# Sums for the second feed-forward layer made and stored in the first, and the embedding's projection moved to the head of the first layer

## The chip, the cores and the metric

The kernel runs on one core of one Trainium2 chip. The metric is the device time of one execution in microseconds (us), as the median of several runs. A profile of one execution gives the instructions of each engine: TensorE (PE: matmuls, PEld: weight loads), VectorE (DVE), ScalarE (ACT), GpSimd (POOL) and SyncE (SP, which here issues every transfer between HBM and SBUF).

## What is computed

An encoder layer over two sequences of 1024 tokens with 1024 features, in float32. Cut to the part that the change touches (attention and the state-space mixer come before it):

```python
h = h + mix @ w_out                                   # "out" product
f = rms_norm(h, g_mlp)
h = h + jnp.square(jax.nn.relu(f @ w_mlp1)) @ w_mlp2  # layer 1 (1024 -> 4096), layer 2 (4096 -> 1024)
e = rms_norm(h, g_ple)
h = h + jax.nn.sigmoid(e @ w_ple_gate) * (p_i @ w_ple_proj)   # gate, and the embedding's projection
return rms_norm(h, g_final)
```

## The kernel before

The two sequences go through three phases. The first two (in-projection, state-space mixer, attention, and a gated unit) take the first 938 us and are not touched. The third, class `PhaseC`, is run once for each sequence, s = 0 and then s = 1, in this order: out product, layer 1, layer 2, gate with the embedding's projection, last norm and output.

**Matmuls in three parts.** Each float32 operand is split into a high and a low part, `hi` by a cast on ACT (L1228), `lo = x - hi` on DVE or POOL (L1229), and a product is made of three matmuls, hi·hi, hi·lo and lo·hi (L461, L462, L463). `split` writes to small buffers of the pool `ops`, three for each of four names, so splits run at most three steps ahead of the matmuls.

**Strassen's products.** Layer 1 goes through eight chunks (`layer1`, ch = 0 to 7) of 512 of the 4096 hidden features. A chunk is seven products of 24 matmuls instead of eight, by the scheme of Strassen and Winograd. The right sides are the normalised activations: half 0 of the tokens directly, and the sums `T` of both halves, which `Sums` makes as the norm of half 1, `norm(h, gb, o, 1)`, comes through transposes on PE (n_ps, L561). In chunk 0 this norm is emitted behind the chunk's first two products (matmuls mz<-act), which need half 0 alone. Each output z (128x1024) is an add on DVE (L1341), a relu (L1346) and a square (L1347) on ACT and a store of 512 KB.

Layer 2 (`strassen`) takes the chunks in pairs (0,1), (2,3), (4,5): a pair is seven products of 48 matmuls; chunk 6 alone is seven of 24, and chunk 7 is plain, 192 matmuls, with the norm for the gate behind it. For a pair, four blocks of hidden values (left, `hid`, 1 MB each) and four of weights (right, `wr`) are loaded; the left sides' four sums are made on DVE and the right sides' four on POOL (L1264), each in two instructions of 128x1024 elements, in place, between the products. DVE also splits the left sides and adds the finished products into h and u2 (L1386, L1395); POOL also splits the right sides.

**The embedding's projection** (pj): p is transposed and split while chunk 7 of layer 2 runs; its 96 matmuls, for each sequence, stand between those of the gate, six for each bank of 128x512. The gate's sigmoid is multiplied by the bank of pj in PSUM (L1537) and added to h (L1538).

**Order.** A scheduler puts each engine's instructions into one order at build time, and each engine then goes through its own in that order. All transfers are issued by SP in one order over eight completion semaphores. `K(R[i], ...)` is one of 16 named places of 8 KB per partition, each with a single tenant at a time; the pool `t2` has two buffers, `up` two, `raw` three, `wp` four, and PSUM's eight banks are split into pm1 (three) and pm2 (five).

Of the kernel before, what the change touches and what calls it, by code (L numbers as in the profile page):

```python
# [16 lines left out]
P = 128  # L17
# [958 lines left out]
class Glu:  # L976


    def __init__(self, nc, tc, ctx, io, ident, ones, scr, B, cols):
        self.nc, self.io, self.ident, self.ones, self.scr, self.B = nc, io, ident, ones, scr, B  # L980

        def pool(name, bufs, **k):
            return ctx.enter_context(tc.tile_pool(name=name, bufs=bufs, reuse_waits="tile", side="right", **k))
        self.one = pool("G1", 1)
        self.two = pool("G2", 2)
        self.cols = cols
        self.w = self.one.tile([P, 4, 512], F32, name="wglu")
        nc.sync.dma_start(out=self.w, in_=io["w_glu"].rearrange("(k p) c -> p k c", p=P))
        self.gt, self.halves = {}, 0
        B.tasks += [self.gelu(), self.unit(0)]  # L990

    def gelu(self):
# [4 lines left out]
        for s in range(2):  # L997
            self.gt[s] = []
            for f in range(4):
                yt = self.two.tile([P, 8, NCK], F32, tag="yt", name="yt")  # L1000
                with B.tc.high_priority(offset=FIRST_AHEAD if s == 0 and f < 2 else 0):
                    nc.sync.dma_start(out=yt, in_=scr["y"][8 * f:8 * f + 8, :, :, s].rearrange("g h t c -> (g h) t c"))
# [177 lines left out]
class PhaseC:  # L1180
# [72 lines left out]
    def strassen(self, A, s1, B, t2, read):  # L1253

        v, g = self.nc.vector, self.nc.gpsimd
        odd = [False]  # L1260

        def op(e, out, x, y, how=ALU.subtract):
            for k in range(0, out.shape[1], 2):
                e.tensor_tensor(*(z[:, k:k + 2] for z in (out, x, y)), op=how)  # L1264

        def product(i, a, b):
            read(i, self.product([a], [b], odd[0]))
            odd[0] = not odd[0]
        product(1, A[0, 0], B[0, 0])
        op(g, B[0, 0], B[0, 1], B[0, 0])  # L1270
        op(g, t2, B[1, 1], B[0, 0])
# [6 lines left out]
        op(g, B[1, 0], B[1, 0], t2)  # L1278
        op(v, A[0, 1], A[0, 1], A[0, 0])
        product(5, s1, B[0, 0])  # L1280
        product(3, A[0, 1], B[1, 1])
        product(7, A[1, 0], B[0, 1])
        product(4, A[1, 1], B[1, 0])
# [30 lines left out]
    def layer1(self, ch, o, hid, norm=None):  # L1314
# [28 lines left out]
        def done(i, l, banks, x):  # L1343
            z = self.t2.tile([P, 2, 512], F32, tag="t2", name="z")
# [3 lines left out]
            nc.sync.dma_start(out=hid[l, :, i], in_=z.rearrange("p f c -> p (f c)"))  # L1348
# [7 lines left out]
        done(0, 0, product(A[0, 1], B21), u)  # L1356
        if norm:

            norm()
# [45 lines left out]

    def run(self, s, x, p, y, first=None):
# [14 lines left out]
        fa = Act(None, ())  # L1421

        for i in range(2):
# [9 lines left out]
            if i == 0:  # L1433
                self.norm(h, gb, self.half(fa, 0, R[0:4]), 0)

# [13 lines left out]
        pairs, h = [], []  # L1449
        for m, i in enumerate((0, 1, 10, 11)):  # L1450
            ht = K(R[i], [2, D], F32, "h")
            nc.sync.dma_start(out=ht, in_=scr["h", s, m])
            pairs.append(ht)
            h += [ht[:, t] for t in range(2)]
        u2 = [self.up.tile([P, 2, 512], F32, tag="u", name="u2") for _ in range(2)]
        for c in range(3):
            A, b = {}, {}
            for j, l, pa_, pb_ in ((0, 0, 6, 2), (1, 0, 7, 3), (0, 1, 8, 4), (1, 1, 9, 5)):
                A[l, j] = K(R[pa_], [4, 512], F32, "hid")
                nc.sync.dma_start(out=A[l, j].rearrange("p k c -> p (k c)"),  # L1460
                                  in_=scr["hid", s, 2 * c + j][l].rearrange("p i c -> p (i c)"))
                r0 = 1024 * c + 512 * j
                b[j, l] = K(R[pb_], [4, 512], F32, "wr")
                nc.sync.dma_start(out=b[j, l], in_=io["w_mlp2"][r0:r0 + 512, 512 * l:512 * l + 512].rearrange("(k p) c -> p k c", p=P))
            self.strassen(A, K(R[12], [4, 512], F32, "s1"), b, K(R[13], [4, 512], F32, "t2"),
                          self.into_h(h, u2, c == 0, False))
        for ch in (6, 7):
            ids = [R[i] for i in ((6, 7, 2, 5) if ch == 6 else (8, 9, 4, 3))]
            hid = []
            for i in range(2):  # L1470
                ht = K(ids[i], [2, 2, 512], F32, "hid")
                nc.sync.dma_start(out=ht.rearrange("p j k c -> p j (k c)"), in_=scr["hid", s, ch][i])
                hid.append(ht)
            b = {}
            for j in range(2):
                for l, w in enumerate(self.rows(nc, io["w_mlp2"], 512 * ch + 256 * j, K, ids[2 + j])):
                    b[j, l] = w
            if ch == 6:
                self.strassen({(i, j): hid[i][:, j] for i in range(2) for j in range(2)},
                              self.sp.tile([P, 2, 512], F32, tag="s", name="s1"), b,  # L1480
                              self.t2.tile([P, 2, 512], F32, tag="t2", name="t2"), self.into_h(h, u2, False, True))
            else:

                pa = {}
                for th in range(2):
                    for k in range(2):
                        pt = self.wp.tile([P, 2, 512], F32R, tag="w", name="pa")
                        pa[th, k] = [pt[:, i] for i in range(2)]
                    for tp in range(2):
                        pp = pm1.tile([P, 2, 2, P], F32, tag="m1", name="pp")  # L1490
                        for t in range(2):
                            pr = self.raw.tile([P, 256], F32, tag="raw", name="pr")
                            nc.sync.dma_start(out=pr, in_=tok_rows(p, 4 * th + 2 * tp + t))
                            for k in range(2):
# [210 lines left out]
```

## Time and profile before

| | |
|---|---|
| median of 3 runs | 2826.99 us (2822.44 to 2829.81) |
| profiled execution | 2826.5 us, span 2824.7 us |
| busy in the span | PE 2531.4 us (90%), DVE 1850.0 (65%), POOL 1357.2 (48%), ACT 1210.5 (43%) |
| mean granted TensorE clock | 0.948 |

The span runs from the first instruction to the last; the 1.8 us beside it lie outside of both. In the rows further down an instruction is given by its line, engine, operation and the names that it writes and reads, then its shapes. "x" is a count, "<-" behind an idle time names what ended it. Matmuls overlap, so that a busy time of 0.39 us for one of 512 columns goes with starts that are closer together.

### The profile page before, as it was taken

The numbers are of one execution on the slowest core, as the hardware profiler recorded it, in microseconds if no ns is written. First come the engines' busy times: TensorE is split into PE (matmuls) and PEld (weight loads), VectorE is DVE, ScalarE is ACT, GpSimd is POOL, SyncE is SP. The second block draws the span as 40 slices with busy tenths as digits, with TensorE's granted clock in tenths as the row PEclk, the third lists the DMA queues.
The fourth block names the chain that finished last, engine by engine and source line by source line (L and its number), as shares of the span: only waits on it lengthen the run. The fifth ranks groups of instructions, "written<-read, shape, count | busy, mean of one in ns | idle before, by whom it ended". The sixth has DMA issues, their size and how long they took to land.

```text
span 2824.7 us, 33883 instructions
## 1 busy us (share of the span) xinstructions
PE 2531.4 (90%) x11822; PEld 1996.8 (71%) x11822; DVE 1850.0 (65%) x2963; ACT 1210.5 (43%) x2306; POOL 1357.2 (48%) x951
## 2 busy tenths in 40 slices
PE   5998878979898988999798899999699999889998
PEld 4876757755565766888576677888588877667686
DVE  4788775667767255554678888553643458888855
ACT  6433323246567334544343334433344444334443
POOL 2223352323331457454557775444754556776642
PEclk9999989989999998999899999999799999999999
DMA  8524544264448513434631230271243362124001
GB/s 282 144 81 117 161 156 125 82 197 141 130 129 278 207 42 102 148 127 134 231 129 60 90 120 25 85 257 47 71 151 112 112 238 97 52 90 149 25 8 60
DMA packets 255499, 352.63 MB, mean 125 GB/s; under 512 B 42448, under 2 KB 184784, under 8 KB 247136
## 3 DMA queue, kind: packets, MB, share of 16 engines
q1 hardware_dynamic: 254240, 350.33, 37.3%
q8 instruction: 93, 1.52, 0.2%
q14 instruction: 78, 0.64, 0.1%
q0 software_dynamic: 1088, 0.14, 0.1%
HBM read 238.58 MB, written 109.60 MB: 123 GB/s over the span
## 4 chain that ended last, share of the span: by engine, by line
PE 65%; DVE 24%; issue 4%; ACT 3%; DMA 2%; POOL 2%; SPq 0%; DVEq 0%; ACTq 0%; POOLq 0%
PE m L462 9%; PE m L463 9%; PE m L461 9%; PE mz L461 7%; PE mz L462 7%; PE mz L463 7%; DVE lo L1229 4%; DVE hid L1264 2%; DVE h L1386 2%; PE ag L461 2%; PE ag L462 2%; PE ag L463 2%; PE glu L1034 2%; PE pss L804 1%; PE po L865 1%
## 5 line engine op out<-in xcount | busy, mean ns | idle before, releaser
L1229 POOL TENSOR_TENSOR lo<-wr,hi 128x512 fp32r<-128x512 f32 x328 | 468.5, 1435 | 471.2 <-ACT hi L1228 384.2
L1228 ACT CAST hi<-wr 128x512 fp32r<-128x512 f32 x328 | 203.3, 621 | 542.8 <-PE m L462 459.3
L462 PE MATMUL m<-hi,lo 128*128 128x512 f32 x912 | 349.1, 412 | 73.8 <-DVE lo L1229 73.6
L1229 POOL TENSOR_TENSOR lo<-w,hi 128x512 fp32r<-128x512 f32 x192 | 263.4, 1378 | 240.0 <-ACT hi L1228 228.2
L463 PE MATMUL m<-lo,hi 128*128 128x512 f32 x912 | 336.5, 407 | 0.0
L1229 DVE TENSOR_TENSOR lo<-hid,hi 128x512 fp32r<-128x512 f32 x200 | 256.6, 1299 | 94.4 <-ACT hi L1228 94.2
L461 PE MATMUL m<-hi 128*128 128x512 f32 x912 | 291.0, 404 | 12.5 <-DVE h L1386 7.5
L462 PEld LDWEIGHTS m<-hi,lo 128*128 128x128 f32 x912 | 177.3, 196 | 128.6 <-DVE lo L1229 93.0
L1228 ACT CAST hi<-w 128x512 fp32r<-128x512 f32 x192 | 117.8, 617 | 238.6 <-PE mz L463 212.9
L461 PEld LDWEIGHTS m<-hi 128*128 128x128 f32 x912 | 176.8, 194 | 57.9 <-DVE h L1386 14.2
L461 PE MATMUL mz<-Th,hi 128*128 128x512 f32 x512 | 200.1, 394 | 16.7 <-ACT Th L1167 16.2
L463 PEld LDWEIGHTS m<-lo,hi 128*128 128x128 f32 x912 | 181.6, 199 | 39.1 <-POOL lo L1229 0.3
L462 PE MATMUL mz<-Th,lo 128*128 128x512 f32 x512 | 200.1, 391 | 0.0
L463 PE MATMUL mz<-Tl,hi 128*128 128x512 f32 x512 | 200.0, 391 | 0.0
L1341 DVE TENSOR_TENSOR z<-u,mz 128x512 f32<-128x512 f32 x128 | 86.6, 683 | 131.9 <-PE mz L463 130.2
L1386 DVE TENSOR_TENSOR h<-h,m 128x512 f32<-128x512 f32 x256 | 158.9, 674 | 3.1 <-PE m L463 3.1
L461 PE MATMUL ag<-acth,whi 128*128 128x512 f32 x384 | 154.6, 404 | 0.9 <-ACT acth L546 0.9
L463 PE MATMUL ag<-actl,whi 128*128 128x512 f32 x384 | 153.3, 404 | 0.0
L462 PE MATMUL ag<-acth,wlo 128*128 128x512 f32 x384 | 152.8, 398 | 0.0
L1341 DVE TENSOR_TENSOR u<-u,mz 128x512 f32<-128x512 f32 x96 | 65.0, 683 | 126.0 <-PE mz L463 126.0
L1228 ACT CAST hi<-hid 128x512 fp32r<-128x512 f32 x200 | 123.5, 617 | 25.1 <-PE m L463 12.8
L461 PEld LDWEIGHTS mz<-Th,hi 128*128 128x128 f32 x512 | 97.2, 190 | 38.0 <-ACT Th L1167 17.0
(384 smaller groups left out, 6121.5 us busy)
## 6 DMA issues: line engine op xcount, KB each, us to landing
w<-in_w_mlp_dram SPq DMA_DIRECT2D x64, 512.0 KB, 4.1
hid<-z SPq DMA_DIRECT2D x64, 512.0 KB, 4.1
hid<-hid SPq DMA_DIRECT2D x32, 1024.0 KB, 6.5
wr<-in_w_mlp_dram SPq DMA_DIRECT2D x32, 1024.0 KB, 5.1
wraw<-in_w_in_dram SPq DMA_DIRECT2D x32, 512.0 KB, 4.7
h<-h SPq DMA_DIRECT2D x16, 1024.0 KB, 5.5
wr<-in_w_out_dram SPq DMA_DIRECT2D x8, 1024.0 KB, 7.3
mix<-ssm SPq DMA_DIRECT2D x8, 1024.0 KB, 10.2
```

Of the source, the lines that this page charges most:

```text
L461: nc.tensor.matmul(out, l[0], r[0], start=first, stop=False)
L462: nc.tensor.matmul(out, l[1], r[0], start=False, stop=False)
L463: nc.tensor.matmul(out, l[0], r[1], start=False, stop=last)
L804: self.nc.tensor.matmul(pss[h][:, u, w], ql, kr, start=True, stop=True)
L865: self.nc.tensor.matmul(po[r, oc], vv[:, r], pts[h][:, sl].rearrange("p a c -> p (a c)"), start=m_ == 0, stop=m_ == len(seq) - 1)
L1034: nc.tensor.matmul(o, self.w[:, k, P * f:P * f + P], gt[k][:, c], start=k == 0, stop=k == 3)
L1228: self.nc.scalar.copy(hi, src)
L1229: lo_eng.tensor_tensor(lo, src, hi.bitcast(F32), op=ALU.subtract)
L1264: e.tensor_tensor(*(z[:, k:k + 2] for z in (out, x, y)), op=how)
L1341: v.tensor_tensor(out[:, f], x[:, f], banks[f], op=ALU.add)
L1386: eng.tensor_tensor(o, o, x, op=ALU.add)
```

## The change

Four things are done for each sequence.

1. The four sums of left sides leave `strassen`. In chunks 0 to 6 `layer1` makes them on DVE from its own outputs (`sub`, four instructions of 128x1024 for each chunk, the same number in all as before), and stores seven operands for each chunk (seven stores of 512 KB instead of four; chunk 7 stores four as before). Outputs z11 and z21 lie in the place R[6], z22 and one sum in R[7].
2. Layer 2 loads the seven left operands of a pair, two transfers of 512 KB each, each operand into a place of its own. The right sides' sums stay on POOL.
3. The embedding's transposes and splits go to the head of the out product (`embedding`), its 96 matmuls directly behind the out product (`embedded`). ACT copies each bank to SBUF, and it is stored (16 stores of 256 KB) and loaded again in the gate (8 loads of 512 KB).
4. The norm of half 1 is emitted ahead of chunk 0, and chunk 0 has the same order of products as the others. (Two loads of the gated unit in the second phase are written at another place in the code, which leaves every engine's order there as it was.)

```diff
-    def strassen(self, A, s1, B, t2, read):
+    def strassen(self, A, B, t2, read):
...
+        def product(i, b):
+            read(i, self.product([left.pop(0)], [b], len(left) % 2))
...
-        product(2, A[0, 1], B[1, 0])
-        op(v, s1, A[1, 0], A[1, 1], ALU.add)
-        op(v, A[1, 0], A[0, 0], A[1, 0])
-        op(v, A[0, 0], s1, A[0, 0])
-        op(g, B[0, 1], B[1, 1], B[0, 1])
-        product(6, A[0, 0], t2)
+        product(2, B[1, 0])
+        op(B[0, 1], B[1, 1], B[0, 1])
+        product(6, t2)
...
-    def layer1(self, ch, o, hid, norm=None):
+    def layer1(self, ch, o, dst, plain):
...
+        def sub(out, x, y, n, op=ALU.subtract):
+            v.tensor_tensor(out, x, y, op=op)
+            store(out, n)
...
+        za = self.K(self.R[6], [2, 2, 512], F32, "za")
+        z11, z21 = za[:, 0], za[:, 1]
+        done(z11, product(A[0, 1], B21), u, 0)
-        if norm:
-
-            norm()
...
-        done(0, 1, p3 if norm else product(A[0, 1], B22, "m1"), u2)
+        done(z21, product(A[0, 1], B22, "m1"), u2, 2 if plain else None)
+        if not plain:
+            sub(new(), z11, z21, 5)
         p7 = product(A[1, 0], o.T[2])
-        done(1, 1, p7, u2)
+        zb = self.K(self.R[7], [2, 2, 512], F32, "zb")
+        z22, sm = zb[:, 0], zb[:, 1]
+        done(z22, p7, u2, 3 if plain else 6)
         add(u, u, p7)
-        done(1, 0, product(A[1, 1], o.T[3]), u)
+        if not plain:
+            sub(sm, z21, z22, 3, ALU.add)
+            s2 = new()
+            sub(s2, sm, z11, 2)
+        z12 = new()
+        done(z12, product(A[1, 1], o.T[3]), u, 1)
+        if not plain:
+            sub(s2, z12, s2, 4)
...
+    def embedded(self, s, pa, wph, wpl):
...
+                for k in range(2):
+                    hi, lo = pa[i, k]
+                    mm3(nc, bank, (hi[:, P * t:P * t + P], lo[:, P * t:P * t + P]), (wph[k][:, c], wpl[l][:, k]), k == 0, k == 1)
+                o2 = self.ops.tile([P, 512], F32, tag=("ah", "al")[l], name="o2")
+                nc.scalar.copy(o2, bank)
+                nc.sync.dma_start(out=self.scr["ple", s][T, :, c], in_=o2)
...
+        self.embedded(s, *emb)
...
+        self.norm(h, gb, o, 1)
         for ch in range(8):
-            self.layer1(ch, o, scr["hid", s, ch], None if ch else lambda: self.norm(h, gb, o, 1))
+            self.layer1(ch, o, scr["op", s, ch], ch == 7)
...
+            def left(n):
+                A[n] = K(R[(0, 2, 8, 9, 15, 6, 7)[n]], [2 * len(chs), 512], F32, "left")
+                for q, ch in enumerate(chs):
+                    nc.sync.dma_start(out=A[n][:, 2 * q:2 * q + 2].rearrange("p k c -> p (k c)"), in_=scr["op", s, ch][n])
```

**PE, where the out product of s = 0 ends and layer 1 begins.** n_ps are the transposes for the norm of half 1, mz<-acth and mz<-actl the products of chunk 0 that need half 0 alone, Th and B the sums and the second half. Before:

```order
L461 MATMUL mz<-acth,hi 128x512
L462 MATMUL mz<-acth,lo 128x512
L463 MATMUL mz<-actl,hi 128x512
L561 MATMUL n_ps<-ident,ft 128x128 x32
L461 MATMUL mz<-Th,hi 128x512 x4
```

The same place in the changed kernel, in two pieces: the end of the projection, and the end of the products of half 0.

```order
L461 MATMUL pj<-wph,pa 128x512
L462 MATMUL pj<-wph,pa 128x512
L463 MATMUL pj<-wpl,pa 128x512
L561 MATMUL n_ps<-ident,ft 128x128 x12
L461 MATMUL mz<-acth,hi 128x512 x4
L561 MATMUL n_ps<-ident,ft 128x128 x4
...
L463 MATMUL mz<-actl,hi 128x512
L561 MATMUL n_ps<-ident,ft 128x128 x8
L461 MATMUL mz<-Th,hi 128x512 x3
```

Before, 48 matmuls of half 0 stood ahead of all 32 transposes (6 of them between those of the out product, 42 behind it). Now 90 matmuls of pj (6 more stand 60 matmuls earlier) are ahead of the first transpose, and the 48 lie between the transposes and the first product that needs T.

**DVE, layer 1, a chunk in the middle of s = 0.** L1361 to L1364 before, L1371 to L1374 now, are the sums of the weights w; z, za, zb are outputs, and mz a finished product. Before:

```order
L1341 TENSOR_TENSOR z<-u_10298,mz 128x512
L1362 TENSOR_TENSOR w_10458<-w_10454,w_10458 128x1024
L1363 TENSOR_TENSOR w_10454<-s_10539,w_10454 128x1024
L1341 TENSOR_TENSOR z<-u_10298,mz 128x512
L1341 TENSOR_TENSOR u<-u,mz 128x512
L1341 TENSOR_TENSOR z<-u_10298,mz 128x512
L1341 TENSOR_TENSOR u<-u,mz 128x512
L1364 TENSOR_TENSOR w_10456<-w_10456,w_10454 128x1024
L1341 TENSOR_TENSOR z<-u,mz 128x512 x2
```

The next chunk in the changed kernel:

```order
L1342 TENSOR_TENSOR za<-u_10568,mz 128x512
L1372 TENSOR_TENSOR w_10736<-w_10732,w_10736 128x1024
L1373 TENSOR_TENSOR w_10732<-s_10817,w_10732 128x1024
L1358 TENSOR_TENSOR z<-za 128x1024
L1342 TENSOR_TENSOR zb<-u_10568,mz 128x512
L1342 TENSOR_TENSOR u<-u,mz 128x512
L1342 TENSOR_TENSOR zb<-u_10568,mz 128x512
L1342 TENSOR_TENSOR u<-u,mz 128x512
L1374 TENSOR_TENSOR w_10734<-w_10734,w_10732 128x1024
L1358 TENSOR_TENSOR zb<-za,zb 128x1024
L1358 TENSOR_TENSOR z<-zb,za 128x1024
L1342 TENSOR_TENSOR z<-u,mz 128x512 x2
```

The four sums (L1358; the fourth stands behind these rows) have come between the adds that take finished products out of PSUM: one ahead of product 7's, two ahead of product 4's.

**DVE, layer 2, the first products of a pair after the first.** Before, with m the finished products:

```order
L1264 TENSOR_TENSOR s_12121<-hid 128x1024
L1229 TENSOR_TENSOR lo<-hid,hi 128x512
L1264 TENSOR_TENSOR s_12121<-hid 128x1024
L1264 TENSOR_TENSOR hid<-hid 128x1024 x2
L1229 TENSOR_TENSOR lo<-hid,hi 128x512
L1264 TENSOR_TENSOR hid<-s_12121,hid 128x1024
L1229 TENSOR_TENSOR lo<-hid,hi 128x512
L1264 TENSOR_TENSOR hid<-s_12121,hid 128x1024
L1229 TENSOR_TENSOR lo<-hid,hi 128x512
```

The changed kernel:

```order
L1411 TENSOR_TENSOR u_11731<-u_11731,m_12443 128x512
L1402 TENSOR_TENSOR h<-h,m_12443 128x512
L1234 TENSOR_TENSOR lo<-left,hi 128x512 x4
L1402 TENSOR_TENSOR h<-h,m_12536 128x512
L1402 TENSOR_TENSOR h<-h,m_12537 128x512
L1402 TENSOR_TENSOR h<-h,m_12538 128x512
L1402 TENSOR_TENSOR h<-h,m_12539 128x512
L1234 TENSOR_TENSOR lo<-left,hi 128x512 x4
```

The sums stood between the splits that the first two products wait for; now splits and adds alone are left there. POOL's order in a pair, right sums and splits, is the same in both kernels.

## Rows read from the trace of the kernel before

**Rows 1.** Windows by stage: busy time of each engine, TensorE's granted clock, DMA share.

```profile
core 0: us, PE busy (x) PEld busy (x) DVE busy (x) ACT busy (x) POOL busy (x), PEclk, DMA share, GB/s
...
1041.50:1073.40 31.90, 7.94 (x34) 5.81 (x33) 28.46 (x38) 14.39 (x25) 21.49 (x13) 0.60 0.07 25
...
1373.80:1477.10 103.30, 84.21 (x342) 66.44 (x341) 77.85 (x82) 38.04 (x67) 61.62 (x37) 0.88 0.38 130
1477.10:1570.80 93.70, 82.78 (x337) 65.60 (x337) 77.56 (x77) 32.80 (x56) 63.95 (x37) 0.93 0.25 90
...
2015.80:2311.80 296.00, 296.00 (x1295) 244.87 (x1296) 121.21 (x143) 133.53 (x184) 157.84 (x115) 0.99 0.43 145
2311.80:2403.80 92.00, 81.70 (x338) 65.45 (x337) 73.89 (x70) 37.51 (x63) 63.57 (x37) 0.94 0.35 122
2403.80:2498.80 95.00, 83.62 (x337) 66.87 (x336) 77.53 (x77) 32.80 (x56) 63.34 (x37) 0.93 0.25 89
...
2592.30:2697.00 104.70, 94.89 (x402) 73.52 (x401) 95.37 (x126) 46.25 (x85) 70.46 (x44) 0.97 0.06 20
```

**Rows 2.** Groups by line, whole span: busy us, mean ns; then idle before and releasers.

```profile
L1229 POOL TENSOR_TENSOR lo<-wr,hi 128x512 fp32r<-128x512 f32 x328 | 468.5, 1435 | 471.2 <-ACT hi L1228 384.2 <-PE m L463 81.5 <-ACT acth L449 5.5
L462 PE MATMUL m<-hi,lo 128*128 128x512 f32 x912 | 349.1, 412 | 73.8 <-DVE lo L1229 73.6
L463 PE MATMUL m<-lo,hi 128*128 128x512 f32 x912 | 336.5, 407 | 0.0
...
L1264 POOL TENSOR_TENSOR wr<-wr 128x1024 f32<-128x1024 f32 x28 | 78.9, 2817 | 0.6
...
L1264 DVE TENSOR_TENSOR hid<-hid 128x1024 f32<-128x1024 f32 x28 | 59.6, 2145 | 0.1
```

**Rows 3.** PE's timeline in the first products of layer 2's second pair, s = 0.

```profile
1484.68 0.50 PE L462 MATMUL m<-hi,lo 128*128 128x512 f32 x1 [0.81 <-DVE lo L1229]
...
1494.10 2.07 PE L462 MATMUL m<-hi,lo 128*128 128x512 f32 x4 [5.50 <-DVE lo L1229]
...
1500.16 1.19 PE L462 MATMUL m<-hi,lo 128*128 128x512 f32 x4 [2.29 <-DVE lo L1229]
```

**Rows 4.** DVE's timeline there.

```profile
1487.88 4.50 DVE L1264 TENSOR_TENSOR hid<-hid 128x1024 f32<-128x1024 f32 x2
1492.30 1.74 DVE L1229 TENSOR_TENSOR lo<-hid,hi 128x512 fp32r<-128x512 f32 x1
...
1504.05 1.21 DVE L1264 TENSOR_TENSOR hid<-hid 128x1024 f32<-128x1024 f32 x1
```

**Rows 5.** POOL's timeline there.

```profile
1475.37 1.29 POOL L1229 TENSOR_TENSOR lo<-wr,hi 128x512 fp32r<-128x512 f32 x1 [1.43 <-ACT hi L1228]
...
1507.48 2.36 POOL L1264 TENSOR_TENSOR wr<-wr 128x1024 f32<-128x1024 f32 x1
1509.80 1.72 POOL L1229 TENSOR_TENSOR lo<-t,hi 128x512 fp32r<-128x512 f32 x1
```

**Rows 6.** PE's timeline at the head of layer 1, s = 0.

```profile
1031.86 0.39 PE L461 MATMUL mz<-acth,hi 128*128 128x512 f32 x1
...
1044.93 3.62 PE L561 MATMUL n_ps<-ident,ft 128*128 128x128 f32 x16 [3.40 <-DVE ft L556]
...
1073.37 2.08 PE L461 MATMUL mz<-Th,hi 128*128 128x512 f32 x4 [8.12 <-ACT Th L1167]
```

**Rows 7.** DVE's timeline in a chunk of layer 1, s = 0.

```profile
1289.86 2.31 DVE L1363 TENSOR_TENSOR w<-s,w 128x1024 f32<-128x1024 f32 x1
1292.10 0.68 DVE L1341 TENSOR_TENSOR z<-u,mz 128x512 f32<-128x512 f32 x1
```

**Rows 8.** ACT's timeline there: the square of z21.

```profile
1289.62 1.06 ACT L1347 ACTIVATE z<-z 128x1024 f32<-128x1024 f32 x1
```

**Rows 9.** Groups by line, DVE: a sum of layer 1's weights.

```profile
L1363 DVE TENSOR_TENSOR w<-s,w 128x1024 f32<-128x1024 f32 x16 | 32.5, 2029 | 1.2
```

**Rows 10.** DMA issues: layer 1's stores; KB each, median us from issue to landing.

```profile
hid<-z SPq DMA_DIRECT2D x64, 512.0 KB, 4.1
```

More of the change, by code (lines that the diff above doesn't have):

```diff
@@ L986, in __init__ @@
         self.cols = cols
+        self.early = [self.input(0, f) for f in range(2)]
         self.w = self.one.tile([P, 4, 512], F32, name="wglu")
@@ L990, in __init__, with input @@
         B.tasks += [self.gelu(), self.unit(0)]
+    def input(self, s, f):
+        yt = self.two.tile([P, 8, NCK], F32, tag="yt", name="yt")
+        self.nc.sync.dma_start(out=yt, in_=self.scr["y"][8 * f:8 * f + 8, :, :, s].rearrange("g h t c -> (g h) t c"))
+        return yt
     def gelu(self):
@@ L999, in gelu @@
             for f in range(4):
[L1000 to L1002 removed]
+                yt = self.early.pop(0) if self.early else self.input(s, f)
                 g_ = self.two.tile([P, S], F32, tag=f"g{f}", name=f"g{f}")
@@ L1341, in add, with done @@
                 v.tensor_tensor(out[:, f], x[:, f], banks[f], op=ALU.add)
-        def done(i, l, banks, x):
-            z = self.t2.tile([P, 2, 512], F32, tag="t2", name="z")
+        def done(z, banks, x, n):
             add(z, x, banks)
@@ L1347, in done, with store, new @@
             nc.scalar.activation(z, z, AF.Square)
-            nc.sync.dma_start(out=hid[l, :, i], in_=z.rearrange("p f c -> p (f c)"))
+            if n is not None:
+                store(z, n)
+        def store(z, n):
+            nc.sync.dma_start(out=dst[n], in_=z.rearrange("p f c -> p (f c)"))
+        def new():
+            return self.t2.tile([P, 2, 512], F32, tag="t2", name="z")
+        def sub(out, x, y, n, op=ALU.subtract):
+            v.tensor_tensor(out, x, y, op=op)
+            store(out, n)
         B11, B21 = ((o.B.hi[kq, 0], o.B.lo[kq, 0]) for kq in range(2))
@@ new lines, in embedded @@
+    def embedded(self, s, pa, wph, wpl):
+        nc = self.nc
+        for T in range(8):
+            i, t = T // 4, T % 4
+            for l in range(2):
+                c = slice(512 * l, 512 * l + 512)
+                bank = self.pm2.tile([P, 512], F32, tag="m2", name="pj")
+                for k in range(2):
+                    hi, lo = pa[i, k]
[3 more added lines that the diff above has]
+                nc.sync.dma_start(out=self.scr["ple", s][T, :, c], in_=o2)
@@ new lines, in run @@
+        hid = []
+        for l in range(2):
+            ht = K(R[2 * l], [2, 2, 512], F32, "hid")
+            nc.sync.dma_start(out=ht.rearrange("p j k c -> p j (k c)"), in_=scr["op", s, 7][2 * l:2 * l + 2].rearrange("j p c -> p j c"))
+            hid.append(ht)
+        b = {}
+        for j in range(2):
+            for l, w in enumerate(self.rows(nc, io["w_mlp2"], 512 * 7 + 256 * j, K, R[(1, 3)[j]])):
+                b[j, l] = w
+        gb = self.gvec(io["g_ple"], D)
+        e = Act(None, ())
@@ L1522, in run @@
+        eids = [[R[i] for i in x] for x in ((8, 9, 10, 11), (0, 2, 1, 3))]
+        for i in range(2):
+            for l in range(2):
+                banks = self.product([hid[i][:, j] for j in range(2)], [b[0, l], b[1, l]])
+                for t in range(4):
+                    o = h[4 * i + t][:, 512 * l:512 * l + 512]
+                    v.tensor_tensor(o, o, banks[t], op=ALU.add)
+            self.norm(h, gb, self.half(e, i, eids[i]), i)
         gf = self.gvec(io["g_final"], D)
-        W = self.square(nc, K, R[12:16], io["w_ple_gate"])
+        W = self.square(nc, K, [R[i] for i in (14, 15, 6, 7)], io["w_ple_gate"])
```

175 lines of the change are left out of this document (74 added, 101 removed).

## The prediction

> **What bounds the kernel now.** The page's shares come first: PE is busy 90% of the span, so what can be won is the time in which it waits. The windows by stage [rows 1] say where. In layer 1 of s = 1, 1295 matmuls take 296.00 us with PE busy throughout, 0.2286 us each; this is the price of a matmul in all that follows (48 are 10.97 us, a pair's 336 are 76.8). Layer 2's pairs take longer than that: 103.30 us for the first of s = 0 (26.5 lost), 93.70 for the second (16.9), 92.00 for the first of s = 1 (15.2), 95.00 for the second (18.2). The two third pairs lose as much as the second ones; I use 17.6 for all four. Chunks 6 and 7 of s = 1 take 104.70 us for 402 matmuls that are worth 91.9 (12.8 lost). And at the head of layer 1 a stretch of 31.90 us has 7.94 us of PE work (24.0 idle); that of s = 1 is the same within 0.1 us.
>
> What ends the waits is read from the groups by line [rows 2]: m<-hi,lo, the matmul that needs a low part first, waited 73.8 us in all, 73.6 of them for DVE's split. m<-lo,hi, which needs POOL's low part too, waited for nothing. So in layer 2 DVE is late and POOL is not. The timelines of one pair show why. PE's three long waits are 0.81, 5.50 and 2.29 us, all in the first two products and all for DVE's lo [rows 3]. The longest ends at 1494.10, when the split that began at 1492.30 is done; ahead of it on DVE stood two sums, 4.50 us [rows 4]. The same sum takes 1.21 us later in the pair, so that about half of that time is DVE waiting while POOL works.
>
> **The change part by part.**
>
> *Head of layer 1.* Out's last matmul ends where the 42 matmuls of half 0 begin, at 1031.86; the transposes begin at 1044.93 and the first product that needs T at 1073.37 [rows 6]. So the norm needs 13.1 us to its first transpose, and 28.4 us from there to T. Now 90 matmuls of pj (20.6 us) cover the first part fully, but the transposes stand behind them in PE's order, 7.5 us later than they could run. From there PE has 32 transposes (3.62 us for 16, so 7.2) and 48 matmuls (11.0) to do, 18.2 us, until T is needed. If the chain still takes 28.4 us, 10.2 of the 24.0 idle stay. It should be shorter, since all four rows of the norm are ready and DVE has no adds of z in between; a chain of 22 us would leave 4. I take 7 left, so 17 won, and 1 for the clock (granted at 0.60 of full in that stretch, [rows 1]). For two sequences **+36**, between 27 and 44.
>
> pj's 96 matmuls cost PE the same in the new place. Their 16 banks are copied on ACT meanwhile, one in 1.37 us. Loads of the first w1 blocks stand behind seven of the 16 stores in SP's order, and the last two behind 15; the latter are needed only by the third product, 18 us after pj.
>
> *Layer 2, later pairs.* 28 DVE instructions for each sequence leave it, so DVE has splits and adds alone. What is late next is POOL, whose order is unchanged: until the first split of t, which the third product needs, it goes through seven splits and seven half sums, from 1475.37 to 1511.52 [rows 5], 36.2 us. PE, not waiting, would want that split 1477.1 + 2 x 10.97 = 1499.0. So POOL was covered by PE's waits for DVE, and this cover goes. Lower bound of its work: eight splits at 1.29 and seven sums at 2.3 [rows 5], 26.4 us, done at 1501.8, PE waits 2.8. Upper bound: as now, done at 1511.5, PE waits 12.5. Of the 9.8 us between, DVE's sums and splits are the cause, some 14 us of work (seven at 1.21 [rows 4] and eight splits at the 0.68 of an add of their size [rows 7]); the splits' 5.4 stay, so 5.4/14 of 9.8, 3.8 us, and a wait of 6.6. One more sum between two splits of t and some clock add 1.4: **8 us lost** for each, 4.2 to 14.4. Four pairs at 17.6 - 8: **+38**.
>
> *First pairs.* s = 1 goes from 15.2 to 8. In s = 0 the last attention tile's transposes stand among the first product's matmuls in both kernels, and their norm on DVE and ACT is not shortened; I leave 4 more, 12. Together **+22**. Chunk 6, with products half as long, keeps about 4 of some 8.5 us: **+9** for both. Chunk 7 has no sums.
>
> *Layer 1.* Each of 14 chunks gets four DVE sums of 1024 columns: 1.21 us alone [rows 4], 2.03 as the like sum of weights has it beside POOL's splits [rows 9]. The first needs z21's square, which ended at 1290.68 [rows 8], before DVE was free of its sum at 1292.1 [rows 7], so it waits for nothing new, and product 7's adds come 1.2 to 2.0 us later than 1292.10. Two more stand ahead of product 4's adds, which were at 1295.9: 3.6 to 6.1 us later in all, so 1299.5 to 1302.0. PE needs their first bank again in the next chunk's second product, 24 matmuls and a few behind the end of product 4 (1296.1 + 6.2 = 1302.3). So the sums just about fit, with the add's own 0.68 us on top. I take 0.65 us for each chunk, **-9**, between 0 and -25.
>
> The Trainium skill has a rule that speaks against this part: in "SBUF — State Buffer", section "SBUF: two separate sides", VectorE with two inputs in SBUF and GpSimd share a port pair that is locked for a whole instruction. By it each of the four sums could wait for a whole split (1.29 us, [rows 5]) first, which makes 2.5 us of each, product 4's adds 7.5 us late, and 1.8 us lost for each chunk, 25 in all: a time of 2751. That two sums took 4.50 us where one takes 1.21 alone [rows 4] agrees with it; that every sum meets a split that has just begun is not what the mean of 2.03 [rows 9] says, so the sum keeps the smaller loss.
>
> The three more stores for each chunk move 1.5 MB more in 38 us, on transfer engines that are 0.43 busy [rows 1] for 4 MB: to about 0.59. They cost PE nothing unless SP gets late (below).
>
> *Smaller ones.* At the end, the last four banks' products and adds no longer run beside pj; about half of eight instructions at 0.68 [rows 7]: **-3**. The embedding's transposes among the out product, and its loads behind the last stores of the sequence before: **-2**.
>
> Sum: 36 + 38 + 22 + 9 - 9 - 3 - 2 = 91. The profiled execution took 2826.5 us, 0.5 under the median, so 2735.5; I say **2735**.
>
> **Rivals.**
>
> *POOL takes DVE's place in layer 2 entirely.* Its seven sums and eight splits keep their 36.2 us, pairs lose 14.4 each (s = 0's first 18), chunk 6 wins 3 in all: 36 + 13 + 9 + 3 - 14 = 47, **2779**. For it: POOL's order is the same, and so are its instructions. Against: half of what lengthens them has gone.
>
> *Layer 1 waits in every chunk.* t2 has two buffers, and z12's adds now need the buffer of z11 - z21, whose store must have landed. Written at 1294, issued at once and landing 4.1 us later [rows 10], it is free at about 1299, 3 us before PE needs the bank. If SP issues it 7 us late, PE loses 4 in each chunk, 56 instead of 9: **2782**. For it: SP has eleven transfers for each chunk instead of eight, in one order. Against: it waits for nothing most of a chunk's 38 us.
>
> *The head isn't covered.* The norm's squares on ACT queue behind copies of pj, or the first w1 blocks come late: 5 won for each sequence instead of 18, **2761**.
>
> *Slower.* The same store wait or the w1 loads queued behind stores in SP's order cost more than a chunk can hide. It decides from (91 + 9)/14 = 7.1 us for each chunk; at 9 us it is 2826.5 - 100 + 126 = **2852**. For it: one queue for all. Against: PE was busy throughout layer 1 [rows 1], with eight transfers for each chunk in the same queue, and DMA has room.
>
> *No change.* DVE's waits return one for one elsewhere, as the splits wait for loads of seven operands instead of four: **2826**. Against: the left operands have seven places of their own, and the transfers' share in the pairs is 0.25 to 0.38 [rows 1].
>
> **How the numbers follow.** The forecast with its bounds (2705 to 2760) gets 0.58; POOL 0.12, layer 1 0.12, the head 0.09, slower 0.06, no change 0.03. The likeliest is 2735. A range that leaves out no more than 2 in 10 takes in the head's case and the nearer halves of POOL's and layer 1's: 2698 to 2780. Within 0.3% is 2818.5 to 2835.5, about what the measurement can tell. Faster by more than that: the forecast and three rivals, less a little for several of them together, 0.90; the same 0.04; slower 0.06.
>
> **What would show it.** Right: PE's wait for DVE's lo in m<-hi,lo falls from 73.6 us to under 15, and m<-lo,hi or m<-hi,lo wait for POOL's lo instead, some 6 us in the third product of each pair; pairs take 82 to 87 us; the stretch between pj's last matmul and the first T product has 4 to 10 us of idle time; layer 1 from its first T product on takes 296 to 310 us; the gate is 20 us shorter. Wrong: layer 1's windows 30 us longer with PE waiting for z or za; pairs over 90 us with POOL without idle time; idle time over 15 us behind pj.

## The result, and the profile after

The changed kernel takes 2730.59 us (median of 4 runs, 2724.92 to 2735.41), the kernel before 2824.72 beside it: a ratio of 0.9665 (0.9639 to 0.9691). Run again later it was 2730.12 against 2822.83, 0.9675 (0.9661 to 0.969). Forecast were 2735 and a range of 2698 to 2780.

The profiled execution took 2731.57 us with a span of 2729.8, 94.9 us less than before. Windows by stage of the changed kernel, which answer to [rows 1]: the head of layer 1 (s = 0), the three pairs of s = 0, then layer 1 and the first two pairs of s = 1.

```profile
core 0: us, PE busy (x) PEld busy (x) DVE busy (x) ACT busy (x) POOL busy (x), PEclk, DMA share, GB/s
1055.90:1082.80 26.90, 14.92 (x81) 12.19 (x79) 25.11 (x23) 13.60 (x25) 25.55 (x15) 0.83 0.22 69
1385.20:1476.10 90.90, 81.22 (x342) 65.20 (x340) 60.12 (x76) 37.31 (x65) 56.36 (x36) 0.92 0.66 247
1476.10:1557.40 81.30, 77.12 (x337) 62.83 (x336) 62.29 (x69) 32.71 (x56) 60.22 (x37) 1.00 0.41 143
1557.40:1640.10 82.70, 78.53 (x337) 63.85 (x336) 61.67 (x70) 32.71 (x56) 59.85 (x37) 0.98 0.23 77
1977.60:2275.70 298.10, 297.41 (x1296) 245.07 (x1297) 170.57 (x174) 133.91 (x189) 175.87 (x116) 0.99 0.50 172
2275.70:2354.10 78.40, 76.87 (x337) 62.66 (x337) 58.86 (x62) 36.15 (x61) 57.34 (x36) 1.00 0.68 259
2354.10:2437.10 83.00, 78.83 (x338) 64.01 (x337) 62.20 (x70) 32.72 (x56) 59.84 (x37) 0.98 0.41 142
```

Every pair is shorter: 103.30 became 90.90, 93.70 became 81.30, and in s = 1 92.00 became 78.40 and 95.00 became 83.00. Layer 1 of s = 1 grew from 296.0 to 298.1. At the head 12.0 us of idle time are left of 24.0.

From the first matmul of a stage to the first of the next one (my sums over the trace's matmuls, us):

| | out to first T | layer 1 | layer 2 | gate to next out, or end |
|---|---|---|---|---|
| before, s = 0 | 135.3 | 300.5 | 395.0 | 112.0 |
| after, s = 0 | 142.6 | 302.4 | 352.9 | 93.0 |
| before, s = 1 | 134.9 | 296.2 | 385.1 | 127.6 |
| after, s = 1 | 146.6 | 298.1 | 344.1 | 110.0 |

Out starts 2.2 us later. So layer 2 gave 83.1 us, layer 1 took 3.8, and all that goes with the projection (out, head, gate, tail and the later start) gave 36.6 - 19.0 - 2.2 = 15.4. These are single executions: in a second one of the changed kernel layer 2 took 356.3 and 340.8 us, the same 697 in all, and out started 0.4 us earlier than before. A difference of 3 us in one stage is thus within the spread, and so is the later start.

PE's groups by line, which answer to [rows 2]:

```profile
L462 PE MATMUL m<-hi,lo 128*128 128x512 f32 x912 | 335.6, 396 | 15.6 <-DVE lo L1234 15.6
L463 PE MATMUL m<-lo,hi 128*128 128x512 f32 x912 | 322.1, 396 | 19.3 <-POOL lo L1234 19.3
...
L461 PE MATMUL mz<-Th,hi 128*128 128x512 f32 x512 | 201.9, 396 | 23.6 <-ACT Th L1172 23.6
```

The wait for DVE's splits fell from 73.6 us to 15.6, and m<-lo,hi, which waited for nothing before, now waits 19.3 us for POOL's. That is the handover that the prediction named. The third row is the head: 11.5 us for each sequence, and little else.

The second pair of s = 0, PE's timeline (as [rows 3]) and then POOL's (as [rows 5]):

```profile
1495.29 0.50 PE L462 MATMUL m<-hi,lo 128*128 128x512 f32 x1 [0.57 <-DVE lo L1234]
1496.42 0.50 PE L463 MATMUL m<-lo,hi 128*128 128x512 f32 x1 [0.62 <-POOL lo L1234]
1504.94 1.20 PE L463 MATMUL m<-lo,hi 128*128 128x512 f32 x4 [2.99 <-POOL lo L1234]
```

```profile
1474.33 1.29 POOL L1234 TENSOR_TENSOR lo<-right,hi 128x512 fp32r<-128x512 f32 x1 [1.43 <-ACT hi L1233]
...
1500.84 2.83 POOL L1269 TENSOR_TENSOR right<-right 128x1024 f32<-128x1024 f32 x1
1503.63 2.95 POOL L1234 TENSOR_TENSOR lo<-t,hi 128x512 fp32r<-128x512 f32 x2
```

The long wait stands in the third product, 2.99 us, and ends when POOL has split t, right behind seven half sums. POOL's way there took from 1474.33 to about 1505, some 30.7 us; 36.2 before, forecast 30.2 (26.4 + 3.8).

The head of layer 1, s = 0, PE's timeline (as [rows 6]):

```profile
1055.91 1.47 PE L561 MATMUL n_ps<-ident,ft 128*128 128x128 f32 x12
...
1082.83 1.22 PE L461 MATMUL mz<-Th,hi 128*128 128x512 f32 x2 [11.46 <-ACT Th L1172]
```

The first transposes run at once behind pj; T comes 26.9 us later, 28.4 before.

A chunk of layer 1, s = 0, DVE's timeline (as [rows 7]):

```profile
1340.54 1.23 DVE L1373 TENSOR_TENSOR w<-s,w 128x1024 f32<-128x1024 f32 x1
1341.90 2.10 DVE L1358 TENSOR_TENSOR z<-za 128x1024 f32<-128x1024 f32 x1
1343.93 0.68 DVE L1342 TENSOR_TENSOR zb<-u,mz 128x512 f32<-128x512 f32 x1
...
1348.39 1.46 DVE L1358 TENSOR_TENSOR zb<-za,zb 128x1024 f32<-128x1024 f32 x1 [0.86 <-ACT zb L1347]
1349.89 2.20 DVE L1358 TENSOR_TENSOR z<-zb,za 128x1024 f32<-128x1024 f32 x1
1352.01 1.27 DVE L1342 TENSOR_TENSOR z<-u,mz 128x512 f32<-128x512 f32 x2
```

The three sums take 2.10, 1.46 and 2.20 us, and product 4's adds come behind them at 1352.01. No wait of PE is put down to them in layer 1.

### The profile page after: what moved, and what is told of

The parts are those of the page before. It is cut to its first block, busy times and chain, and to the rows that moved or that the text cites. A ratio compares the mean times of both kernels' runs of the same rounds, so it can differ in the third digit from the quotient of the medians.

```text
span 2729.8 us, 34325 instructions
## 1 busy us (share of the span) xinstructions
PE 2497.1 (91%) x11822; PEld 1974.4 (72%) x11822; DVE 1853.0 (68%) x2963; ACT 1219.7 (45%) x2338; POOL 1363.5 (50%) x951
## 4 chain that ended last, share of the span: by engine, by line
PE 67%; DVE 17%; DMA 5%; issue 4%; ACT 3%; POOL 3%; SPq 0%; DVEq 0%; ACTq 0%; POOLq 0%
PE m L463 10%; PE m L462 10%; PE m L461 10%; PE mz L463 7%; PE mz L462 6%; PE mz L461 6%; PE ag L463 2%; PE ag L462 2%; PE ag L461 2%; PE glu L1039 2%; DVE h L1402 1%; PE pss L804 1%; PE po L865 1%; PE pt L844 1%; DVE lo L1234 1%
## 5 line engine op out<-in xcount | busy, mean ns | idle before, releaser
L1234 POOL TENSOR_TENSOR lo<-w,hi 128x512 fp32r<-128x512 f32 x192 | 282.5, 1483 | 199.4 <-ACT hi L1233 198.2
L1234 DVE TENSOR_TENSOR lo<-left,hi 128x512 fp32r<-128x512 f32 x196 | 266.1, 1377 | 128.7 <-ACT hi L1233 128.5
L1234 POOL TENSOR_TENSOR lo<-wr,hi 128x512 fp32r<-128x512 f32 x160 | 227.7, 1434 | 249.2 <-ACT hi L1233 228.7
L462 PE MATMUL m<-hi,lo 128*128 128x512 f32 x912 | 335.6, 396 | 15.6 <-DVE lo L1234 15.6
L463 PE MATMUL m<-lo,hi 128*128 128x512 f32 x912 | 322.1, 396 | 19.3 <-POOL lo L1234 19.3
L1234 POOL TENSOR_TENSOR lo<-right,hi 128x512 fp32r<-128x512 f32 x168 | 233.8, 1398 | 165.3 <-ACT hi L1233 154.6
L1233 ACT CAST hi<-right 128x512 fp32r<-128x512 f32 x168 | 104.4, 622 | 266.9 <-PE m L462 223.4
L463 PEld LDWEIGHTS m<-lo,hi 128*128 128x128 f32 x912 | 173.0, 190 | 59.9 <-POOL lo L1234 24.3
L1233 ACT CAST hi<-wr 128x512 fp32r<-128x512 f32 x160 | 99.1, 620 | 211.3 <-PE m L462 201.8
L1233 ACT CAST hi<-left 128x512 fp32r<-128x512 f32 x196 | 121.2, 619 | 25.9 <-PE m L463 20.9
```

What stands on the lines that cost most here:

```text
L462: nc.tensor.matmul(out, l[1], r[0], start=False, stop=False)
L463: nc.tensor.matmul(out, l[0], r[1], start=False, stop=last)
L1233: self.nc.scalar.copy(hi, src)
L1234: lo_eng.tensor_tensor(lo, src, hi.bitcast(F32), op=ALU.subtract)
```

## The experiments

**The projection alone.** The kernel before with the projection's part of the change:

```diff
+        emb = self.embedding(p, s)
...
+        self.embedded(s, *emb)
...
+        self.norm(h, gb, o, 1)
         for ch in range(8):
-            self.layer1(ch, o, scr["hid", s, ch], None if ch else lambda: self.norm(h, gb, o, 1))
+            self.layer1(ch, o, scr["hid", s, ch])
```

> The kernel before with only the embedding's projection moved to the head of layer 1 (and the norm of half 1 ahead of chunk 0). Theory: the two parts of the change add up; the head wins what pj covers less the transposes' delay, so layer 2 loses its 100 us as before, and the whole is 15 to 25 us faster than before. Idle time of PE between pj and the first T product some 12 us for each sequence. Rival (the parts need each other: the place of the projection costs layer 2 or layer 1 something, or pays only with the new operands): under 8 us faster, or slower.

Measured: 2797.60 us against 2821.92, a ratio of 0.9914 (0.9899 to 0.9928), 24.3 us faster, at the upper end of the theory. 11.7 of them stand in layer 2, but only 5.6 in chunk 7, from which the embedding's transposes and splits have gone; the other 6, in the pairs and chunk 6, were not followed up.

**The sums alone.** The changed kernel without `embedding` and `embedded`, and with before's lines for them in chunk 7 and in the gate:

```diff
-        emb = self.embedding(p, s)
-        self.embedded(s, *emb)
```

> The changed kernel with the embedding's projection back in its old places (chunk 7 of layer 2, and between the gate's matmuls). Theory: the sums alone win what layer 2 shows, 70 to 82 us against before, and layer 1 from its first T product takes the 300.4 and 296.0 us of before, since its 3.7 us more in the changed kernel are half clock behind the head's wait and not the four sums. Rival (layer 1 pays for the sums): layer 1 keeps 302 and 298 us or more.

Measured: 2744.06 us against 2821.92, 0.9726 (0.9711 to 0.974), 77.9 us faster. Layer 1 from its first T product, windows of s = 0 and s = 1:

```profile
1070.00:1370.00 300.00, 299.87 (x1325) 247.60 (x1325) 201.75 (x265) 139.73 (x208) 172.56 (x115) 0.99 0.53 184
1971.40:2267.60 296.20, 296.16 (x1297) 244.90 (x1298) 170.94 (x174) 133.16 (x187) 175.47 (x115) 0.99 0.49 172
```

300.0 and 296.2 us are before's lengths, though DVE is busy 171 us instead of 121 in that of s = 1. So layer 1 pays nothing for the sums, and the 3.8 us that it lost in the changed kernel come with the projection. The projection alone shows them too (298.2 us in s = 1). The two parts sum to 102 us, the change gives some 93: layer 2 wins 79.7 with the sums alone, 11.7 with the projection alone, 83.1 with both. Clearing chunk 7 wins 4.1 us beside the sums and 5.6 without them; the rest of the shortfall is those other 6 us, which don't come back beside the sums, and its cause stays open. Between the two executions of the changed kernel, too, a single pair differs by up to 1.6 us.

**The norm ahead of the projection.**

```diff
-        self.embedded(s, *emb)
...
         self.norm(h, gb, o, 1)
+        self.embedded(s, *emb)
```

> The changed kernel with the norm of half 1 written ahead of the projection, so that the order has 59 matmuls of pj, 12 transposes, 19 of pj, 4 transposes, 12 of pj and then the rest. Theory (what is left at the head is that T's chain of about 26 us starts only behind pj): the chain starts some 7 us earlier, PE's idle time ahead of T falls from 12 to 4 or 5 us for each sequence, and the kernel is 12 to 20 us faster than the changed one. Rival (the chain is held by copies of pj on ACT, or by POOL, and not by the transposes' place): the chain gets longer by as much, within 5 us of the changed kernel.

Measured: 2725.84 us against 2821.92, 0.9654 (0.9629 to 0.9679): by its median 4.8 us under the changed kernel's, by the ratios to the kernel before some 3 us, in intervals that overlap. In the profile the stages out and layer 1 are 7.4 us shorter for both sequences together. Neither side is right alone. The transposes begin 8.0 us earlier, but T only 3.1 us (1079.75), so the chain has grown to 31.8 us. PE's waits there, and DVE's:

```profile
1061.91 0.50 PE L462 MATMUL mz<-acth,lo 128*128 128x512 f32 x1 [1.81 <-POOL lo L1234]
1079.75 0.58 PE L461 MATMUL mz<-Th,hi 128*128 128x512 f32 x1 [4.99 <-ACT Th L1172]
```

```profile
1066.63 1.73 DVE L1371 TENSOR_TENSOR s<-w,w 128x1024 f32<-128x1024 f32 x1 [3.62 <-DMA w<-in_w_mlp_dram]
```

DVE stood 3.62 us for a block of w1, with the norm's next steps queued behind; the chain grew by 4.9. The block's buffer (`wp`, four of them) is that of an operand of pj, so its load can't begin before pj ends; the trace names the load, and that the buffer is what delays it is read from the code.

**Layer 1's sums twice.**

```diff
             v.tensor_tensor(out, x, y, op=op)
+            if n != 4:
+                v.tensor_tensor(out, x, y, op=op)
             store(out, n)
```

> The changed kernel with three of layer 1's four sums made twice in each chunk (the same values written again), those that stand ahead of product 4's adds on DVE: 3.6 to 6.1 us more on DVE for each of 14 chunks. By the prediction's price the sums just fit, with 0 to 3 us to spare, so PE now waits 1 to 5 us for each chunk: 15 to 70 us slower than the changed kernel, 40 as the middle. Rival (layer 1 has room that the price did not see): within 8 us of the changed kernel.

Measured: 2743.77 us against 2821.92, 0.9729 (0.9712 to 0.9745), 13 us over the changed kernel by the medians and 18 by the ratios: at the theory's low end or just under it, and over the rival's 8. Window of layer 1, s = 1, and PE's waits in it:

```profile
1975.20:2280.80 305.60, 298.36 (x1297) 243.87 (x1298) 209.09 (x195) 133.89 (x189) 186.00 (x116) 0.99 0.48 167
```

```profile
PE mz L461 <- DVE z L1342: 6.6, 6, 1.5
```

DVE worked 38.5 us more, 5.5 for each of the seven chunks, and PE waits 1.1 us in six of them, for product 4's adds. One of these chunks, DVE's timeline and then PE's; L1360 are the sums made again:

```profile
2128.36 2.20 DVE L1360 TENSOR_TENSOR zb<-za,zb 128x1024 f32<-128x1024 f32 x1
2130.60 2.19 DVE L1358 TENSOR_TENSOR z<-zb,za 128x1024 f32<-128x1024 f32 x1
2132.71 1.27 DVE L1342 TENSOR_TENSOR z<-u,mz 128x512 f32<-128x512 f32 x2
2133.91 1.21 DVE L1360 TENSOR_TENSOR z<-zb,za 128x1024 f32<-128x1024 f32 x1
```

```profile
2133.44 0.50 PE L461 MATMUL mz<-acth,hi 128*128 128x512 f32 x1 [1.13 <-DVE z L1342]
```

The last repeated sum has come behind product 4's adds, so not all of the 5.5 us delays them. The room can be read directly: in the changed kernel the same chunk has its first add at 2129.45, done at 2130.1, and the matmul that waits here starts at 2132.27, 2.1 us later.

```profile
2129.45 1.27 DVE L1342 TENSOR_TENSOR z<-u,mz 128x512 f32<-128x512 f32 x2
2132.27 0.39 PE L461 MATMUL mz<-acth,hi 128*128 128x512 f32 x1
```

Over all 14 chunks it is 2.0 to 2.9 us: inside the 0 to 3 of the price, and not wide.

**A right sum on DVE.**

```diff
-        op(B[0, 1], B[1, 1], B[0, 1])
...
+        op(B[0, 1], B[1, 1], B[0, 1], self.nc.vector)
         product(3, B[1, 1])
```

> The changed kernel with one of the four right sums of layer 2 (its two instructions stand on POOL ahead of the first split of t) on DVE instead, which the scheduler puts among the first two products. Theory (POOL's chain of splits and sums to t's first split is what the third product now waits for): that chain is some 5 us shorter on POOL and DVE needs 2.4 us for the same sums, so the third product's loss of 3.3 to 4.9 us goes and pairs lose 2 to 3.5 us instead of 5 to 6.8: 10 to 20 us faster than the changed kernel. Rival (the two engines exclude each other, so a sum costs the chain the same wherever it stands, or delays DVE's splits): within 5 us of the changed kernel, the loss moved to the second product.

Measured: 2732.30 us against 2824.71, 0.9673 (0.9658 to 0.9687): the changed kernel's time, and the rival's case. PE's waits in the three pairs of s = 1:

```profile
PE m L462 <- DVE lo L1234: 5.2, 3, 2.3
PE m L461 <- DVE h L1402: 1.8, 4, 0.7
PE m L463 <- POOL lo L1234: 0.5, 1, 0.5
```

In the changed kernel the same stretch has 8.7 us for POOL's splits and 1.2 for DVE's. POOL's wait has all but gone and DVE's has come back in its place: the second and third pair lose 5.7 us in the second product instead of 1.9 and 4.9 in the second and third.

**Without the right sums.**

```diff
         product(1, B[0, 0])
-        op(B[0, 0], B[0, 1], B[0, 0])
-        op(t2, B[1, 1], B[0, 0])
         product(2, B[1, 0])
-        op(B[0, 1], B[1, 1], B[0, 1])
-        product(6, t2)
-        op(B[1, 0], B[1, 0], t2)
+        product(6, B[0, 1])
```

> The changed kernel without layer 2's right sums: the seven products use the blocks of weights as they are, so layer 2's values are others. Theory (POOL's sums are what is left of a pair's loss, with the lock that they hold against DVE's splits): pairs lose under 1.5 us, 25 to 30 us faster than the changed kernel. Rival (DVE's adds and splits or the operands' loads are next): pairs still lose 4 us or more.

Measured: 2697.71 us against 2824.71, 0.9552 (0.9538 to 0.9567), some 33 us under the changed kernel, a little more than expected. The second pair of s = 0:

```profile
1475.00:1551.20 76.20, 76.20 (x338) 63.10 (x337) 55.03 (x70) 31.98 (x56) 36.63 (x28) 1.00 0.42 151
```

76.20 us with PE busy throughout, and so are five of six pairs: the right sums are all that was left there. DVE, with the same instructions as in the changed kernel, is busy 55.0 us instead of 62.3; over all of layer 2 its splits take 1.14 us each instead of 1.38.

The sixth, the first pair of s = 0, got no shorter: 92.9 us against 91.1. PE's wait for the attention tile's rows, in the changed kernel and then here:

```profile
1409.49 1.11 PE L573 MATMUL n_ps<-ident,att 128*128 128x128 f32 x4 [4.05 <-DVE att L570]
```

```profile
1408.96 1.11 PE L573 MATMUL n_ps<-ident,att 128*128 128x128 f32 x4 [11.25 <-DVE att L570]
```

The tile holds this pair whatever the right sums do; the waits for splits lie underneath.

**The other sequence's tiles earlier.**

```diff
-                for T in range(ch - 1, ch + ch // 7):
+                for T in {1: (0, 1), 6: (6, 7), 7: ()}.get(ch, (ch,)):
```

> The changed kernel with the attention tiles of the other sequence's norm, which go one for each chunk of layer 1 of s = 0, started one tile earlier, so that none is left for layer 2's first pair. Theory (the first pair of s = 0 loses 14.7 us where that of s = 1 loses 2.4 because the last tile's transposes stand in it): its loss falls to 2 to 5 us, 10 to 12 us faster than the changed kernel. Rival (it is late operands: transfers are busiest there, share 0.66): the loss stays over 10 us.

Measured: 2733.19 us against 2824.71, 0.9683 (0.9667 to 0.9699), no gain. Layer 1 and the first pair of s = 0:

```profile
1082.00:1388.80 306.80, 303.01 (x1329) 248.11 (x1330) 205.84 (x277) 141.83 (x213) 169.35 (x114) 0.99 0.54 187
1388.80:1474.10 85.30, 79.43 (x337) 64.80 (x336) 56.80 (x62) 36.10 (x61) 59.13 (x37) 0.96 0.65 248
```

The pair is 5.6 us shorter than the changed kernel's 90.90, with a wait for POOL's split of 5.40 us in the third product where the tile's transposes had stood in the second. It still loses some 9 us, between what the theory and the rival had. So the two causes cover each other: with the tile and no right sums the pair loses as much as with both, and with the tile gone POOL's chain still makes 9 us of the 15. Layer 1 is 4.4 us longer; 2.6 of them are two waits of PE for the tile's rows, which now fall there.

**Three together** (norm ahead, sum on DVE, tiles earlier).

> The norm written ahead of the projection, the right sum on DVE and the tiles earlier, all three on the changed kernel. Theory: each takes its loss from another stage, so the gains add: 8 for the head, 10 to 20 for the right sum, 10 to 12 for the tiles, 25 to 40 us faster than the changed kernel, near 2695. Rival (they meet at layer 1's or layer 2's beginning, or the right sum wins nothing): under 20 us.

Measured: 2720.62 us against 2824.71, 0.9628 (0.9613 to 0.9643), some 10 us under the changed kernel: the rival, and two of the three win nothing alone. In the trace out and layer 1 give 5.5 us and layer 2 gives 6.0. The first pair of s = 0 takes 81.2 us, where the sum on DVE alone leaves it at 90.0 and the earlier tiles alone at 85.5.

**The right sums kept.** The sums of weights are the same for both sequences, so s = 0 stores them and s = 1 loads them as operands; the norm stands ahead of the projection.

```diff
+            if s == 0:
...
+                self.strassen(A, b, K(R[14], [nq, 512], F32, "t2"), read, keep)
+                continue
...
+            o[6] = operand(6, 14)
...
+            self.strassen(A, B, None, read, None)
```

> The norm ahead of the projection, and layer 2's right sums, which are sums of weights and so the same for both sequences, stored by s = 0 as it makes them and loaded by s = 1 as operands, so that s = 1 has no sums in layer 2 at all. Theory (POOL's sums are the whole of what the pairs still lose): the three pairs of s = 1 lose under 1 us each instead of 2.4, 6.8 and 6.7, chunk 6 some 3 less, layer 2 of s = 1 takes 324 to 328 us instead of 344; with 8 us of the head 20 to 28 us faster than the changed kernel. Rival (28 more transfers in the one queue, s = 0's stores and s = 1's loads, come late): PE waits for operands, under 10 us faster or slower.

> The changed kernel itself once more, on the same chip and beside the same runs of the kernel before: 0.966 to 0.969 of before by all theories. It gives the spread against which gains of some us are read.

Measured side by side: 2705.14 us (2701.36 to 2707.95), 0.9581 (0.9568 to 0.9594), and 2730.12 for the changed kernel, 0.9675 (0.9661 to 0.969). 25.0 us faster, as expected, and better than both kernels. The second pair of s = 1:

```profile
2342.50:2418.60 76.10, 76.10 (x337) 63.03 (x336) 54.96 (x69) 31.96 (x56) 36.65 (x28) 1.00 0.52 193
```

83.00 us became 76.10, with no wait; the first pair still loses 1.5. Layer 2 of s = 1 took 328.2 us (344.1 and 340.8 in the changed kernel's two executions), and out and layer 1 are 11 us shorter. The transfers in the one queue are 25 more and not 28, since 7 loads of weights fall away beside 32 new ones; they cost PE nothing that shows.

## Why the prediction was right, point by point

**The sum held because two errors met.** The terms of layer 2 came to 69 us and measured 83. Head, tail and the small terms came to 36 - 3 - 2 = 31 and measured 15.4. Layer 1 came to -9 and measured -3.8. That they cancelled was luck.

**The signs that the prediction named.** PE's wait for DVE's splits was to fall under 15 us and fell to 15.6; the wait in the third product was to be some 6 us and is 3.0; the later pairs were to take 82 to 87 us and take 81.3 to 83.0, the first ones 90.9 and 78.4; 4 to 10 us were to be idle at the head and 12.0 are; the gate was to be 20 us shorter and is 19.0 and, with the tail, 17.6. Layer 1, 302.4 and 298.1, lies inside its 296 to 310. The direction held for each, the sizes for about half.

**Layer 2, the mechanism.** Right, and shown: DVE's sums held the splits (the sums alone win 77.9 us), and POOL's chain is late next (without the right sums five pairs lose nothing). The bounds of 4.2 to 14.4 us (the upper one's terms add up to 13.9) held for the four later pairs, which lose 5.1 to 6.8 where 8 were taken. A loss is counted here against 76.2 us, what a pair takes in which PE never waits; the price of layer 1 made it 76.8. The later pairs gave 47 us instead of 38, the first pairs 26 instead of 22, chunk 6 5.8 instead of 9, and chunk 7, which had no term, 4.2.

POOL's chain itself was right within a microsecond, in part by luck: the 9.8 us above its bare work were put down to DVE alone, but 1.2 of them were a wait for PE.

```profile
1502.43 1.66 POOL L1229 TENSOR_TENSOR lo<-wr,hi 128x512 fp32r<-128x512 f32 x1 [1.18 <-PE m L463]
```

PE came for t's split some 3.7 us later than I had it, since its second product loses 1.9 us and eight matmuls of the third that need none of POOL's low part come first.

**First pairs.** That of s = 1 loses 2.4 us and not 8: there the term was mis-sized. POOL's first sum starts there 3.1 us ahead of PE's first product, in the second pair of s = 0 only 0.6; that no pair ahead of it holds the places is read from the code. That of s = 0 loses 14.7 instead of 12. The 4 us left for the attention tile were added to POOL's 8, but the tile's wait lies over those for splits and does not add to them: without the right sums the pair loses as much.

**The head** is the term that failed by most: 7 us of idle time were to be left, 12.0 are. The chain to T took 26.9 us, inside 22 to 28.4. Behind the 7 us stood a chain of 25.2, so 1.7 of the 5 missing are the chain's. The other 3.3 are the work put against it, 18.2 us where 14.9 were done: "32 transposes (3.62 us for 16, so 7.2)", but twelve now take 1.47 us. The 3.62 us of [rows 6] stand in a stretch with a granted clock of 0.60 (0.58 in the row itself) and with waits on either side, so the row wasn't the price of the work at full clock. And the clock gave nothing back: layer 1 starts behind an idle stretch as before and is 1.9 us longer for each sequence, while it has before's length in the kernel with the sums alone. Its first 10 us in the kernel before, and in the changed kernel:

```profile
1073.40:1078.00 4.60, 4.60 (x11) 3.67 (x12) 3.73 (x3) 0.92 (x2) 4.60 (x4) 0.50 0.38 114
1078.00:1083.00 5.00, 5.00 (x22) 4.08 (x21) 0.00 (x0) 0.94 (x2) 5.00 (x5) 0.93 0.30 85
```

```profile
1082.80:1088.00 5.20, 4.52 (x9) 2.69 (x10) 2.91 (x4) 2.02 (x4) 5.20 (x5) 0.50 0.31 85
1088.00:1093.00 5.00, 5.00 (x17) 3.96 (x17) 1.29 (x2) 2.98 (x4) 5.00 (x5) 0.72 0.11 27
```

The granted clock is at the lower of its two levels, 1.2 GHz, longer than before, and about 0.6 us of the 1.9 are two short waits right behind T. With 5 us of idle time in place of 11.5 (norm ahead) layer 1 takes 300.4 and 296.7 us. So the 1 us taken as won for the clock was a loss of some 1.3, or 1.9 with these waits.

**The small terms** -3 and -2 were small for what they stood for. PE waited 4.7 us (s = 0) and 2.8 (s = 1) for rows of p that the embedding's transposes need; the tail, 17.6 us shorter, gave 4.2 less than the 21.8 of pj's 96 matmuls.

**Layer 1.** "The sums just about fit" was right, with 2.0 to 2.9 us of room, but one step to it was not. The three sums ahead of product 4's adds take 5.9 us on average (2.2, 1.5 and 2.2), and behind the first chunk the adds come 6.2 to 6.6 us later than before, just over the price's upper end. PE needs the bank later than I had it: 39 matmuls into the next chunk instead of "24 matmuls and a few", at 1305.7 and not 1302.3 in the chunk of [rows 7]. With that no chunk loses anything to the sums; the 3.8 us come with the head.

By the Trainium skill ("SBUF — State Buffer", section "SBUF: two separate sides") a VectorE instruction with two inputs in SBUF and a GpSimd instruction that reads SBUF lock each other out for a whole instruction. I had made 2.5 us of each sum by it. Two of the four take 2.2 us on average and the other two 1.5, where one takes 1.21 alone [rows 4]; all four together come to 1.86, nearer to the 2.03 of [rows 9] than to 2.5. The longer ones agree with such a lock, though no wait in the trace names it. The 1.8 us lost for each chunk, which I had worked out from it, did not come, and by these figures would not have come with 2.5 either, as the bank is needed 3.4 us later.

**The rivals.** POOL did take DVE's place, for 19.3 of 73.6 us, and not for all. No wait of layer 1 on a store reached PE; DVE did wait for one, up to 3.7 us at a time in s = 1, ahead of the chunk's last sum, where nobody waited for it. Of SP's queue being too slow no run showed anything, with 25 transfers more either. The head's rival took 5 us won for each sequence; the idle time fell by 12.0, less the 1.9 behind it. The splits did not wait for loads of the seven operands: without the right sums PE is busy throughout in five pairs.

## What to carry to other kernels

When an engine's waits all name one other engine, ask what a third engine has been doing under the cover of those waits: its time to the same point, less what the first one had slowed it by, is the next limit, and here it came out within a microsecond, with some luck. Work that doesn't depend on the sequence is better made once and stored: here, on the engine that was late or moved to its neighbour, the same sum cost the same. Two waits of one stage need not add: one can lie under the other, and taking away either alone then wins little. And price work from a row in a stretch at full clock; a short group between two waits is no price.

## What the runs showed that was not expected

A sum that changes engines can change nothing: with one right sum on DVE the pair's loss went from (1.9, 4.9) to 5.7 us in the second product, a pair 82.0 instead of 83.0 us, and the changed kernel itself took 81.3 there in its second execution. Two readings are left, which no run here separates. DVE goes through its own instructions in order, and the sum's halves, 2.07 us each on average, stand ahead of splits. Or the two engines take turns, as the exclusive lock of the Trainium skill has it ("SBUF — State Buffer", section "SBUF: two separate sides"); that DVE's splits are shortened by what POOL leaves out (62.3 to 55.0 us with the same instructions) agrees with that.

With idle stretches of about 5 us in place of 11.5 the layer behind them was 1.4 to 2.0 us shorter (300.4 and 296.7 us against 302.4 and 298.1). It still began at a lower clock, 0.60 and 0.50 in its first 4.3 us, as the kernel before did behind its longer stretches.
